# A hybrid diffusion backbone on one core: products over the whole array, and modulation as row sums on VectorE

## Chip, cores and metric

One core of one Trainium2 chip runs the program. The metric is device time in microseconds for one execution; lower is better.

## What is computed

Two layers work on 512 latent tokens and 256 context tokens of 1024 channels. Each layer is modulated by six vectors of 1024 values, made from a conditioning vector c for the latent tokens and c_ctx for the context tokens:

```
mod   = silu(c) @ ada_w + ada_b                    # 6 x 1024, per layer; and with c_ctx
h     = rms_norm(x, g1) * (1 + scale1) + shift1
att   = window_attention(rope(q), rope(k), v, ctx keys and values, sink)
mls   = mlstm_bidir(q, k, v, gates)                # chunks of 128, forward and backward
hy    = hyena(short_conv(u), filters)              # filters: a small network, times exp(-t*delta)
x     = x + gate1 * ((sum_r sigmoid(g_r) * (branch_r @ w_branch_r)) @ w_out)
h2    = rms_norm(x, g2) * (1 + scale2) + shift2
x     = x + gate2 * ((silu(conv3(h2 @ w_up)) * conv3(...)) @ w_down)
```

The last layer needs no context output; there only shift and scale of the first norm are used for c_ctx. The output is a final RMSNorm of the latent tokens.

## The kernel before

Activations lie channel-major, `[128 channels, tokens]`, in eight tiles. Every large matrix product is made of fp32r parts: an operand is split in a high part (ScalarE copies it, line 339) and a low part (VectorE subtracts, line 340), and `kstep` (line 401) issues three matmuls per 128 channels: high by high, high by low, low by high. A weight tile of 128x1024 fp32 (512 KB) comes on the SP queue into one of four buffers `wr` and is split into one of three `wh` and one of three `wl`. The split has raised priority.

**The order of work.** The large products are one stream. Everything else is written as generators ("lanes") that `spawn` adds with a rate; after each `kstep`, `tick` advances a clock and lets each lane take steps in proportion. `finish` runs out what is left at a stage's end. A scheduler then places the instructions of each engine in one fixed order; every engine works through its own in order. Per layer the stages are: projections of the gates (pool `mixa`, with the Hyena filters of layer 0 and the modulation beside them), attention projections and attention beside mLSTM projections (`mix`), mLSTM beside Hyena's projections, Hyena and the merge of the branches (`mixe`), and output projection with the feed-forward part (`ffn`). The filters of layer 1 run in layer 0's feed-forward part. Tiles of two kinds, `T` and `H`, are counted for each stage in `SIZES`.

**Modulation** (`ada`, lines 465 to 490). A block is 512 of the 6144 values. Eight matmuls put two silu vectors (stationary, 32 columns, line 473) against 128x512 of `ada_w`, four groups of channels side by side in the array's columns; ScalarE copies the sum (477), four transposes turn it (481), VectorE adds the groups (484) and the bias (485). There are 12 blocks per layer: four before the first product, eight in layer 0's first projections, nine of layer 1 in layer 0's feed-forward part and three in layer 1's projections.

**Scores** (`scores`, lines 1037 and 1038). For every block of 128 queries and head a product with the key's high part takes all 128 rows (the query's 64 high channels over its 64 low ones); a second one with the key's low part takes the 64 rows of the head's group. An item (a block, two heads, one group; 24 in layer 0 and 16 in layer 1) writes one score tile of three PSUM banks, of which there is one. Masks are added by bf16 products (1049).

**Filter taps** (`filter_taps`, 654 and 655): a product of 128 rows with the high part of w3, and one of 64 rows with its low part. **Decays** (`ml_mix`, 1351 and 1353): two products of 64 rows, with the high and the low part of a running maximum, then a mask.

Of the kernel before, what the change touches and what calls it, by code (L numbers as in the profile page):

```python
# [20 lines left out]
P = 128  # L21
# [11 lines left out]
# order of the m-tiles of the stacked [D_MODEL, 128] weights of a layer  # L33
# [12 lines left out]
# columns of the packed per-channel vectors of a layer  # L46
# [11 lines left out]
# ---------------------------------------------------------------- constants of the shapes  # L58
# [70 lines left out]
# ---------------------------------------------------------------- layout of the inputs  # L129
# [12 lines left out]
def _layout(inp):  # L142
# [7 lines left out]
    out["adaw"] = a["ada_w"].reshape(DEPTH, 4, 2, P, 12, 512).transpose(0, 4, 1, 3, 2, 5).reshape(DEPTH, 12, 4, P, 1024)  # L150
# [88 lines left out]
class Prog:  # L239
# [3 lines left out]
    SIZES = {'A0': (18, 26), 'A1': (8, 41), 'mix': (20, 21), 'E': (16, 29), 'ffn0': (20, 23), 'ffn1': (30, 0)}  # L243
# [12 lines left out]
    ADA1 = 9  # L256
# [4 lines left out]
    def __init__(self, tc, es, aps, dbg=None):  # L261
# [18 lines left out]
        self.nident = c.tile([64, 64], F32R, name="nident")  # L280
        nc.vector.tensor_scalar(self.nident, self.ident[:64, :64], -1.0, None, op0=ALU.mult)
# [6 lines left out]
        self.rope = c.tile([P, 2, SEQ], F32, name="rope")  # L288
# [3 lines left out]
        self.sil = c.tile([P, KD, 32], F32, name="sil")  # L292
        self.g_dram = {}

    def load_consts(self):
        nc, a = self.nc, self.a
        nc.gpsimd.dma_start(self.sv[1], a["sv"][1])
        nc.gpsimd.dma_start(self.fg, a["fg"])
        nc.gpsimd.dma_start(self.rope, a["rope"].rearrange("s p t -> p s t"))
        nc.gpsimd.dma_start(self.maskb, a["masks"])  # L300

    # ---- small helpers
# [39 lines left out]
    # ---- weaving of the mixers' work into the stream of matrix products  # L342
    def spawn(self, rate, *gens):
        lane = Lane(rate, gens)
        lane.t0 = self.clock
# [23 lines left out]
    def fill(self, n):  # L369
        """work put by for the places where the products have to wait"""  # L370
        for _ in range(n):
            next(self.spare, None)

    def finish(self, what=""):
        left = 0.0
        while self.lanes:
            for lane in self.lanes:
                c = lane.step()
                left += c or 0.0
# [4 lines left out]
    # ---- GEMM  # L384
# [34 lines left out]
    def proj_first(self, l, ms, parts):  # L419
        """three m-tiles, part by part, two of them k outermost: the operands may still be coming"""  # L420
# [44 lines left out]
    def ada(self, l, blocks):  # L465
        """blocks of 512 of the six vectors; the groups of k-tiles side by side in the array's columns"""
        nc = self.nc
        for b in blocks:
            ps = self.M("adap")
            for q in range(2):  # L470
                aw = [self.raw(self.a["adaw"][l, b, 2 * q + j]) for j in range(2)]
# [13 lines left out]
            nc.vector.tensor_tensor(m, m, self.svs(l, "adab", b * 4, 4).unsqueeze(2).to_broadcast([P, 4, 2]), op=ALU.add)  # L485
            for i, base in ((1, 0), (2, 24)):
                for h in range(2):
                    if b == (2 if i == 1 else 8) + h:
                        g = self.svs(l, f"n{i}g", 4 * h, 4).unsqueeze(2).to_broadcast([P, 4, 2])
                        nc.vector.scalar_tensor_tensor(self.A[l, i][:, 4 * h:4 * h + 4, :], m, 1.0, g, op0=ALU.add, op1=ALU.mult)  # L490

    # ---- norms
# [56 lines left out]
    # ---- Hyena filters in the frequency domain  # L549
# [20 lines left out]
    def filters(self, l, L, resident, overlap):  # L570
        """spectra of the filters, by order and half of the channels: filter taps, then their DFT"""
# [1198 lines left out]
```

## Time and profile before

| | |
|---|---|
| time, median of 3 runs (lowest to highest) | 2808.58 us (2805.72 to 2810.65) |
| span of the profiled execution | 2804.0 us; its own time is not listed apart |
| TensorE, VectorE, ScalarE, GpSimd busy | 2695.0, 1752.1, 1051.3, 282.1 us |
| weight loads for modulation | 96 of 512 KB |
| moved by DMA | 347.66 MB |

The page gives per engine the time in which it was busy, and lines give groups of instructions by the line of the kernel, with output and inputs by the program's names (`pg` is the PSUM tile of the large products, `wh`, `wl` the weight's parts, `s` scores, `x`, `xl` the parts of queries and keys, `adap`, `adaq` modulation sums). Matmuls overlap, so a busy TensorE is not the same as one at its peak; for what an instruction holds the stream, the distance between two starts in the timeline is read. The kernel's span starts at the first instruction; a run's time includes what lies around it.

### The profile page before, as it was taken

Reading aid. Unit: us, or ns where it says so; the run is one execution under the profiler, and the core shown is the slowest. Engines: PE = TensorE matmul, PEld = TensorE weight load, DVE = VectorE, ACT = ScalarE, POOL = GpSimd, SP = SyncE. Lnnn points to the kernel's source line nnn. Section 1 sums busy time; section 2 is a strip of 40 time slices with the busy share of each in tenths; the row PEclk is TensorE's granted clock in tenths of the full one; section 3 lists DMA queues with packets and bytes.
Section 4 is the critical chain, followed back from the end, with each engine's and each line's share of the span. In section 5 each row is a group of like instructions: output and inputs, shape, how many; then the busy total and the mean of one; then the engine's idle time right before and its main releaser. Section 6 shows DMA issues by size and latency. Waiting matters only on the chain. (4 is left out here: it accounts for less than half of the span.)

```text
span 2804.0 us, 38203 instructions
## 1 busy us (share of the span) xinstructions
PE 2695.0 (96%) x14762; PEld 2199.1 (78%) x14762; DVE 1752.1 (62%) x3076; ACT 1051.3 (37%) x1893; POOL 282.1 (10%) x297
## 2 busy tenths in 40 slices
PE   6899999999999998999999999999999999999998
PEld 2678787778888886787888887777787778888887
DVE  5685554556457765767667566655447477665666
ACT  4344343445323233433233234534345233533333
POOL 3241110000000301011101000210000002000000
PEclk8999999999999999999999999999999999999999
DMA  7555331122436542354443224541222556333332
GB/s 257 168 199 195 108 95 38 38 66 91 151 130 207 174 155 70 116 169 143 132 131 91 68 65 149 185 136 40 76 91 94 185 183 211 98 98 98 97 95 65
DMA packets 153158, 347.66 MB, mean 124 GB/s; under 512 B 15553, under 2 KB 52910, under 8 KB 152976
## 3 DMA queue, kind: packets, MB, share of 16 engines
q1 hardware_dynamic: 132976, 319.03, 34.3%
q0 software_dynamic: 20000, 26.19, 3.7%
q8 instruction: 117, 1.92, 0.3%
q14 instruction: 65, 0.53, 0.1%
HBM read 287.02 MB, written 52.17 MB: 121 GB/s over the span
## 5 line engine op out<-in xcount | busy, mean ns | idle before, releaser
L401 PE MATMUL pg<-hh,wh 128*128 128x512 f32 (+1 forms) x2536 | 923.8, 365 | 7.9 <-ACT hh L339 6.2
L401 PE MATMUL pg<-hlo,wh 128*128 128x512 f32 (+1 forms) x2536 | 900.7, 355 | 4.1 <-DVE hlo L340 3.9
L401 PE MATMUL pg<-hh,wl 128*128 128x512 f32 (+1 forms) x2536 | 898.6, 355 | 0.1
L340 DVE TENSOR_TENSOR wl<-wr,wh 128x1024 fp32r<-128x1024 f32 x294 | 370.3, 1260 | 304.1 <-ACT wh L339 296.2
L401 PEld LDWEIGHTS pg<-hh,wh 128*128 128x128 f32 x2536 | 483.4, 191 | 94.5 <-issue 26.7
L401 PEld LDWEIGHTS pg<-hlo,wh 128*128 128x128 f32 x2536 | 484.3, 191 | 67.2 <-DVE hlo L340 6.8
L401 PEld LDWEIGHTS pg<-hh,wl 128*128 128x128 f32 x2536 | 483.1, 191 | 66.2 <-issue 1.5
L339 ACT CAST wh<-wr 128x1024 fp32r<-128x1024 f32 x294 | 308.8, 1050 | 567.2 <-PE pg L401 525.3
L1527 DVE SCALAR_TENSOR_TENSOR x<-pg,mod,x 128x512 f32<-128x512 f32 (+1 forms) x242 | 149.0, 629 | 113.2 <-PE pg L401 111.0
L401 PE MATMUL pg<-fh,wh 128*128 128x512 f32 (+1 forms) x544 | 194.0, 358 | 8.7 <-DVE x L1527 8.0
L401 PE MATMUL pg<-fl,wh 128*128 128x512 f32 (+1 forms) x544 | 191.6, 352 | 0.0
L401 PE MATMUL pg<-fh,wl 128*128 128x512 f32 (+1 forms) x544 | 190.5, 351 | 0.9 <-DVE wl L340 0.9
L742 ACT ACTIVATE u<-pg,sv 128x512 f32<-128x512 f32 (+1 forms) x165 | 116.6, 708 | 134.9 <-PE pg L401 134.8
L743 DVE SCALAR_TENSOR_TENSOR u<-pg,sv,u 128x511 f32<-128x511 f32 (+1 forms) x165 | 108.3, 658 | 86.2 <-ACT u L742 86.0
L401 PEld LDWEIGHTS pg<-fh,wh 128*128 128x128 f32 x544 | 103.7, 191 | 29.2 <-DVE x L1527 12.1
L1067 ACT ACTIVATE p<-s,sm 128x512 f32<-128x512 f32 (+2 forms) x80 | 55.3, 692 | 171.8 <-DVE sm L1064 142.9
L1063 DVE TENSOR_REDUCE sm<-s 128x1 f32<-128x512 f32 (+2 forms) x80 | 55.2, 690 | 99.5 <-PE s L1049 67.8
L401 PE MATMUL pg<-bh,wh 128*128 128x512 f32 (+1 forms) x320 | 111.7, 381 | 5.6 <-ACT bh L339 3.3
L401 PEld LDWEIGHTS pg<-fh,wl 128*128 128x128 f32 x544 | 103.7, 191 | 15.1 <-DVE wl L340 1.4
L401 PEld LDWEIGHTS pg<-fl,wh 128*128 128x128 f32 x544 | 103.9, 191 | 14.0 <-issue 0.7
L744 DVE SCALAR_TENSOR_TENSOR u<-pg,sv,u 128x511 f32<-128x511 f32 (+1 forms) x165 | 108.7, 660 | 2.5
L401 PE MATMUL pg<-bh,wl 128*128 128x512 f32 (+1 forms) x256 | 94.7, 370 | 0.0
(301 smaller groups left out, 4068.3 us busy)
## 6 DMA issues: line engine op xcount, KB each, us to landing
wr<-in_wA SPq DMA_DIRECT2D x222, 512.0 KB, 3.7
wr<-in_adaw SPq DMA_DIRECT2D x96, 512.0 KB, 4.6
wr<-in_wD SPq DMA_DIRECT2D x48, 512.0 KB, 3.6
wr<-in_wB SPq DMA_DIRECT2D x24, 512.0 KB, 5.2
gates<-gt SPq DMA_DIRECT2D x28, 384.0 KB, 2.7
gc<-in_g POOLq DMA_DIRECT2D x40, 256.0 KB, 3.8
g<-gd SPq DMA_DIRECT2D x40, 256.0 KB, 4.3
g<-gates SPq DMA_DIRECT2D x24, 384.0 KB, 7.7
```

Source lines behind the costliest of these rows:

```text
L339: nc.scalar.copy(h, src)
L340: (nc.gpsimd if pool else nc.vector).tensor_tensor(l, src, h.bitcast(F32), op=ALU.subtract)
L401: self.nc.tensor.matmul(ps[:, :hi - lo], a[:, ks], b[:, lo:hi], start=(first and i == 0), stop=(last and i == 2))
L742: nc.scalar.activation(dst[:, lo:hi], ps[:, :n], AF.Identity, bias=b, scale=w(1))
L743: V(dst[:, lo + 1:hi], ps[:, 0:n - 1], w(0), dst[:, lo + 1:hi], op0=mul, op1=add)
L744: V(dst[:, lo:hi - 1], ps[:, 1:n], w(2), dst[:, lo:hi - 1], op0=mul, op1=add)
L1063: nc.vector.tensor_reduce(sm[:, j:j + 1], src, axis=AX.X, op=ALU.max)
L1067: nc.scalar.activation(t[:, :w], src, AF.Exp, bias=sm[:, 2 + j:3 + j], scale=0.125, accum_out=sm[:, 4 + j:5 + j])
L1527: self.nc.vector.scalar_tensor_tensor(x[m][:, lo:hi], ps[:, :hi - lo], self.mod[l][:, p * 8 + m, j:j + 1], x[m][:, lo:hi], op0=ALU.mult, o ...
```

## The change

Four parts.

*Modulation.* The first four blocks of layer 0 stay as they are. The other 20 use `ada_w` transposed: a tile holds 128 output values as rows of 1024 inputs, and one VectorE instruction per vector multiplies it by silu(c), which stands in all partitions (`silb`), and sums each row into `mod`. Layer 0's blocks and layer 1's first four do so for two vectors, layer 1's last eight for one. The product for the first of two vectors goes into a buffer of tag `wl`, the last one over the tile itself. These lanes stay alive over the stage's ends until the feed-forward part.

*Whole array.* The key's low part is put twice, over both halves of the partitions, as the high part was; the second score product then takes all rows. The taps' second product takes all 128 rows of hd. The maximum's high and low parts share one tile of 128 rows, and `nident` is two negated identities above each other.

*Room.* `silb` takes 8 KB per partition; rope moves from a constant to two `H` tiles that are loaded in each layer's attention projection; `SIZES` gets smaller.

```diff
-    out["adaw"] = a["ada_w"].reshape(DEPTH, 4, 2, P, 12, 512).transpose(0, 4, 1, 3, 2, 5).reshape(DEPTH, 12, 4, P, 1024)
+    out["adaw"] = a["ada_w"][0, :, :2048].reshape(4, 2, P, 4, 512).transpose(3, 0, 2, 1, 4).reshape(4, 4, P, 1024)
+    out["adat"] = a["ada_w"].transpose(0, 2, 1).reshape(DEPTH * 48, P, 1024)[16:]
+    out["cb"] = np.stack([a["c"][0], a["c_ctx"]])
...
-    SIZES = {'A0': (18, 26), 'A1': (8, 41), 'mix': (20, 21), 'E': (16, 29), 'ffn0': (20, 23), 'ffn1': (30, 0)}
+    SIZES = {'A0': (18, 23), 'A1': (8, 38), 'mix': (20, 19), 'E': (16, 27), 'ffn0': (20, 21), 'ffn1': (28, 0)}
...
+        self.nident = c.tile([P, 64], F32R, name="nident")
+        for h in (0, 64):
+            nc.vector.tensor_scalar(self.nident[h:h + 64, :], self.ident[h:h + 64, h:h + 64], -1.0, None, op0=ALU.mult)
...
+    def ada_rows(self, l, blocks):
+        nc = self.nc
+        for b in blocks:
+            n = 2 if l < DEPTH - 1 or b < 4 else 1
+            for c in range(4):
+                aw = self.raw(self.a["adat"][l * 48 + b * 4 + c - 16])
+                for v in range(n):
+                    prod = aw
+                    if v < n - 1:
+                        prod = self.wp.tile([P, 1024], F32R, tag="wl", name=self.uid("wl"), bufs=self.WB[1])
+                    nc.vector.scalar_tensor_tensor(prod, aw, 1.0, self.silb[:, v, :], op0=ALU.mult, op1=ALU.mult,
+                                                   accum_out=self.mod[l][:, b * 4 + c, v:v + 1])
+                if c < 3:
+                    yield 1.0
+            self.ada_end(l, b, n)
+            yield 1.0
+
+    def silu_rows(self):
+        nc = self.nc
+        nc.gpsimd.dma_start(self.silb.rearrange("p v k -> p (v k)"), self.a["cb"].rearrange("v k -> (v k)").partition_broadcast(P))
+        for v in range(2):
+            s = self.silb[:, v, :]
+            t = self.wp.tile([P, 1024], F32, tag="wr", name=self.uid("wr"), bufs=self.WB[0])
+            nc.scalar.activation(t, s, AF.Tanh, scale=0.5)
+            nc.vector.scalar_tensor_tensor(s, t, 1.0, s, op0=ALU.add, op1=ALU.mult)
+            nc.vector.tensor_scalar(s, s, 0.5, None, op0=ALU.mult)
...
-                nc.tensor.matmul(ps, hd[0:64, t * P:(t + 1) * P], w3l[0:64], start=False, stop=True)
+                nc.tensor.matmul(ps, hd[:, t * P:(t + 1) * P], w3l, start=False, stop=True)
...
+        self.rope = [self.H("rope") for _ in range(2)]
+        for i in range(2):
+            self.nc.gpsimd.dma_start(self.rope[i], self.a["rope"][i])
...
         if key:
-            nc.gpsimd.dma_start(top[64:128, :n], top[0:64, :n])
-            nc.gpsimd.dma_start(bot[0:64, :n], bot[64:128, :n])
-            return top, bot, low
+            for a, b in ((top, bot), lows):
+                nc.gpsimd.dma_start(a[64:128, :n], a[0:64, :n])
+                nc.gpsimd.dma_start(b[0:64, :n], b[64:128, :n])
+            return (top, bot), lows
...
-                nc.tensor.matmul(ps[:, o:o + n], qh[ds_, self.chunk(qb)], kl[ds_, ks], start=False, stop=stop)
+                nc.tensor.matmul(ps[:, o:o + n], qh[:, self.chunk(qb)], kl[:, ks], start=False, stop=stop)
...
-                    for x in range(2):
-                        nc.tensor.matmul(pt[:, :w * P], self.nident[:, r:r + 1].to_broadcast([64, P]),
-                                         mn[x][:, i * P:(i + w) * P], start=(x == 0), stop=False)
+                    nc.tensor.matmul(pt[:, :w * P], self.nident[:, r:r + 1].to_broadcast([P, P]),
+                                     mn[:, i * P:(i + w) * P], start=True, stop=False)
...
-                    self.spawn(R["ada"], self.ada(0, range(4, 12)))
+                    self.silu_rows()
+                    self.spawn(1 / 15, self.ada_rows(0, range(4, 12)), stays=True)
...
-                    self.spawn(R["ada"], self.ada(l, range(self.ADA1, 12)))
+                    self.spawn(1 / 11, self.ada_rows(l, range(4, 12)), stays=True)
...
+            self.finish("all")
...
-                    self.spawn(self.RATE[1]["ada"], self.ada(1, range(0, self.ADA1)))
+                    self.spawn(1 / 28, self.ada_rows(1, range(0, 4)))
```

The order in which the engines get their instructions moves with it. On VectorE, in layer 0's first projections, where the second filter's taps (`ht`) are made and the first filter's spectrum (`glo`, `ghi`) is written, the kernel before has this; line 664 starts the next norm of a filter:

```order
L642 TENSOR_TENSOR ht_781<-pm_747,dec_371 128x512
L340 TENSOR_TENSOR wl_890<-wr_887,wh_889 128x1024
L722 TENSOR_TENSOR glo_797<-pe_711,pp_715 128x512
L723 TENSOR_TENSOR ghi_798<-pe_711,pp_715 128x256
L724 TENSOR_TENSOR ghi_798<-pp_715,pe_711 128x256
L642 TENSOR_TENSOR ht_812<-pm_786,dec_373 128x512
```

and the changed one this, at the same place (line 343 is the low part, 681 the taps, 761 to 763 the spectrum, 514 the row sums):

```order
L514 SCALAR_TENSOR_TENSOR wl_672,mod_89<-wr_670,silb 128x1024
L681 TENSOR_TENSOR ht_757<-pm_723,dec_372 128x512
L514 SCALAR_TENSOR_TENSOR wr_670,mod_89<-wr_670,silb 128x1024
L761 TENSOR_TENSOR glo_771<-pe_687,pp_691 128x512
L762 TENSOR_TENSOR ghi_772<-pe_687,pp_691 128x256
L763 TENSOR_TENSOR ghi_772<-pp_691,pe_687 128x256
L343 TENSOR_TENSOR wl_848<-wr_845,wh_847 128x1024
L681 TENSOR_TENSOR ht_786<-pm_762,dec_374 128x512
L514 SCALAR_TENSOR_TENSOR wl_927,mod_89<-wr_925,silb 128x1024
```

The row sums stand one by one between taps, spectrum and the weights' low parts.

On TensorE, in the attention of layer 0, an item's scores were (of the kernel before; `xl` is the key's low part):

```order
L1037 MATMUL s_679_3350<-x_630_3069,x_640_3145 128x256
L1038 MATMUL s_679_3350<-xl_3071,x_640_3145 128x256
L1037 MATMUL s_679_3350<-x_630_3069,x_650_3221 128x256
L1038 MATMUL s_679_3350<-xl_3071,x_650_3221 128x256
L1037 MATMUL s_679_3350<-x_630_3069,x_640_3145 128x256
```

and are now:

```order
L1081 MATMUL s_656_3229<-x_602_2935,x_613_3014 128x256
L1082 MATMUL s_656_3229<-xl_2937,x_613_3014 128x256
L1081 MATMUL s_656_3229<-x_602_2935,x_625_3095 128x256
L1082 MATMUL s_656_3229<-xl_2937,x_625_3095 128x256
L1081 MATMUL s_656_3229<-x_602_2935,x_613_3014 128x256
```

Nothing moves there; only the rows that the second product takes differ, which these lines don't print.

On VectorE near the start of the program, ahead of the first weights' low parts (`wl`), stands in the changed kernel what makes silu:

```order
L495 TENSOR_TENSOR mod_89<-mod_89,sv_85 128x8
L528 SCALAR_TENSOR_TENSOR silb<-wr_462,silb 128x1024
L528 SCALAR_TENSOR_TENSOR silb<-wr_466,silb 128x1024
L529 TENSOR_SCALAR silb<-silb 128x1024 x2
L343 TENSOR_TENSOR w3l_379<-w_99_376,w3h_378 128x512
```

In the kernel before the modulation's bias (485) is followed there by the low part of w3 at once.

## Rows read from the trace of the kernel before

**Rows 1.** Page: busy time of each engine, share of the span, instructions.
```profile
PE 2695.0 (96%) x14762; PEld 2199.1 (78%) x14762; DVE 1752.1 (62%) x3076; ACT 1051.3 (37%) x1893; POOL 282.1 (10%) x297
```

**Rows 2.** Stretches: length; busy us (instructions) of PE, PEld, DVE, ACT, POOL; granted clock; DMA.
```profile
35.00:315.00 280.00, 256.63 (x1387) 187.58 (x1386) 196.67 (x310) 111.86 (x185) 78.54 (x66) 0.94 0.56 189
360.00:595.00 235.00, 234.89 (x1370) 180.22 (x1369) 124.12 (x284) 91.65 (x250) 10.07 (x19) 1.00 0.20 59
1085.00:1735.00 650.00, 633.33 (x3578) 529.58 (x3576) 447.79 (x670) 230.70 (x320) 63.86 (x63) 0.98 0.36 113
```

**Rows 3.** Timeline of TensorE, the stream: start, us, engine, line, operation, tiles, shape, count.
```profile
391.51 0.28 PE L401 MATMUL pg<-hlo,wh 128*128 128x256 f32 x1
391.63 0.28 PE L401 MATMUL pg<-hh,wl 128*128 128x256 f32 x1
...
607.26 0.39 PE L401 MATMUL pg<-hlo,wh 128*128 128x512 f32 x1
607.49 0.40 PE L401 MATMUL pg<-hh,wl 128*128 128x512 f32 x1
```

**Rows 4.** Timeline of TensorE, modulation: products of a half block; transposes.
```profile
1261.90 0.39 PE L401 MATMUL pg<-hh,wl 128*128 128x512 f32 x1
1262.22 1.06 PE L473 MATMUL adap<-wr,sil 128*32 128x512 f32 x8
...
1263.56 0.39 PE L401 MATMUL pg<-hlo,wh 128*128 128x512 f32 x1
...
1281.90 0.28 PE L401 MATMUL pg<-hh,wl 128*128 128x256 f32 x1
1282.02 0.60 PE L481 MATMUL adaq<-ident,adae 128*128 128x128 f32 x4
1282.58 0.28 PE L401 MATMUL pg<-hlo,wh 128*128 128x256 f32 x1
```

**Rows 5.** Timeline of TensorE, scores in layer 0's attention.
```profile
392.43 0.38 PE L1038 MATMUL s<-xl,x 64*128 64x256 f32 x1
392.74 0.39 PE L1037 MATMUL s<-x,x 128*128 128x256 f32 x1
```

**Rows 6.** Groups of TensorE by form: count, busy us, mean ns, idle before.
```profile
L1037 PE MATMUL s<-x,x 128*128 128x256 f32 x112 | 40.5, 361 | 1.5 <-DMA x<-xl 1.4
...
L655 PE MATMUL pm<-w3l,hd 64*128 64x512 f32 x40 | 20.5, 528 | 0.9 <-DVE w3l L340 0.9
...
L1037 PE MATMUL s<-x,x 128*128 128x384 f32 x32 | 13.8, 431 | 0.0
```

**Rows 7.** Timeline of TensorE, a pair of taps in the stream.
```profile
113.73 0.28 PE L401 MATMUL pm<-hh,wl 128*128 128x256 f32 x1
...
114.82 0.28 PE L401 MATMUL pm<-hlo,wh 128*128 128x256 f32 x1
```

**Rows 8.** Timeline of TensorE, a decay in the stream.
```profile
607.81 0.73 PE L1351 MATMUL pm<-mn,nident 64*128 64x512 f32 x2
...
608.94 0.39 PE L401 MATMUL pg<-hlo,wh 128*128 128x512 f32 x1
```

**Rows 9.** Groups of VectorE by form, the nearest to a row sum: mean ns after the bar.
```profile
L340 DVE TENSOR_TENSOR wl<-wr,wh 128x1024 fp32r<-128x1024 f32 x294 | 370.3, 1260 | 304.1 <-ACT wh L339 296.2 <-PE pg L401 2.8 <-ACT o L1126 1.1
...
L1063 DVE TENSOR_REDUCE sm<-s 128x1 f32<-128x640 f32 x32 | 26.4, 824 | 45.0 <-PE s L1049 34.3 <-ACT p L1067 10.7
...
L1599 DVE SCALAR_TENSOR_TENSOR u<-t,u 128x768 f32<-128x768 f32 x22 | 21.4, 971 | 1.6 <-ACT t L1598 1.4
```

**Rows 10.** Groups of ScalarE: the read of an accumulator.
```profile
L1067 ACT ACTIVATION_READ_ACCUMULATOR p<-s,sm 128x1 f32 x80 | 15.7, 196 | 0.0
```

**Rows 11.** Timeline of ScalarE near the start; idle before, what ended it.
```profile
53.56 0.62 ACT L339 CAST w3h<-w 128x512 fp32r<-128x512 f32 x1 [3.48 <-DMA w<-in_hw]
```

**Rows 12.** Waits of TensorE: us in total, times, longest.
```profile
PE adaq L481 <- ACT adae L477: 12.5, 5, 6.0
...
PE pg L401 <- DVE wl L340: 0.9, 1, 0.9
```

More of the change, by code (lines that the diff above doesn't have):

```diff
@@ L255 @@
     NTAIL = 2
-    ADA1 = 9
     ADDS = 6
@@ L287, in __init__ @@
         self.fg = c.tile([P, KD], F32, name="fg")
-        self.rope = c.tile([P, 2, SEQ], F32, name="rope")
         self.maskb = c.tile([P, 2, P], BF16, name="maskb")
@@ L292, in __init__ @@
         self.sil = c.tile([P, KD, 32], F32, name="sil")
+        self.silb = c.tile([P, 2, D], F32, name="silb")
         self.g_dram = {}
@@ L340, in split, with spawn @@
         (nc.gpsimd if pool else nc.vector).tensor_tensor(l, src, h.bitcast(F32), op=ALU.subtract)
-    def spawn(self, rate, *gens):
+    def spawn(self, rate, *gens, stays=False):
         lane = Lane(rate, gens)
+        lane.stays = stays
         lane.t0 = self.clock
@@ L375, in finish @@
         left = 0.0
-        while self.lanes:
+        while any(what == "all" or not x.stays for x in self.lanes):
             for lane in self.lanes:
-                c = lane.step()
-                left += c or 0.0
+                if what == "all" or not lane.stays:
+                    c = lane.step()
+                    left += c or 0.0
             self.lanes = [x for x in self.lanes if x.gens]
@@ L470, in ada @@
             for q in range(2):
-                aw = [self.raw(self.a["adaw"][l, b, 2 * q + j]) for j in range(2)]
+                aw = [self.raw(self.a["adaw"][b, 2 * q + j]) for j in range(2)]
                 for g in range(4):
@@ L484, in ada @@
             nc.vector.tensor_reduce(m, p2.rearrange("p (c g r) -> p c r g", g=4, r=32)[:, :, 0:2, :], axis=AX.X, op=ALU.add)
[L485 to L490, printed above, removed]
+            self.ada_end(l, b, 2)
@@ new lines, in ada_end @@
+    def ada_end(self, l, b, n):
+        nc = self.nc
+        m = self.mod[l][:, b * 4:b * 4 + 4, 0:n]
+        nc.vector.tensor_tensor(m, m, self.svs(l, "adab", b * 4, 4).unsqueeze(2).to_broadcast([P, 4, n]), op=ALU.add)
+        for i in (1, 2):
+            for h in range(2):
+                if b == (2 if i == 1 else 8) + h:
+                    g = self.svs(l, f"n{i}g", 4 * h, 4).unsqueeze(2).to_broadcast([P, 4, n])
+                    nc.vector.scalar_tensor_tensor(self.A[l, i][:, 4 * h:4 * h + 4, 0:n], m, 1.0, g, op0=ALU.add, op1=ALU.mult)
@@ L776, in att_finish @@
         self.att["q"].append(self.stacked(self.att_last[0], self.parts(l)[-1][1], False))
+        self.rope = None
     def rope_swap(self, q):
@@ L787, in rope_add @@
         nc = self.nc
-        nc.gpsimd.tensor_tensor(r, r, self.rope[:, 1, :], op=ALU.mult)
-        nc.vector.tensor_tensor(q[:, :SEQ], q[:, :SEQ], self.rope[:, 0, :], op=ALU.mult)
+        nc.gpsimd.tensor_tensor(r, r, self.rope[1], op=ALU.mult)
+        nc.vector.tensor_tensor(q[:, :SEQ], q[:, :SEQ], self.rope[0], op=ALU.mult)
         nc.vector.tensor_tensor(q[:, :SEQ], q[:, :SEQ], r, op=ALU.add)
@@ L796, in stacked @@
         top, bot, low = self.T("x0", dt=F32R), self.T("x1", dt=F32R), self.T("xl", dt=F32R)
-        for h, t in ((0, top), (64, bot)):
+        lows = (low, self.T("xm", dt=F32R)) if key else (low, low)
+        for h, t, lw in ((0, top, lows[0]), (64, bot, lows[1])):
             nc.scalar.copy(t[h:h + 64, :n], x[h:h + 64, :n])
-            nc.vector.tensor_tensor(low[h:h + 64, :n], x[h:h + 64, :n], t[h:h + 64, :n].bitcast(F32), op=ALU.subtract)
+            nc.vector.tensor_tensor(lw[h:h + 64, :n], x[h:h + 64, :n], t[h:h + 64, :n].bitcast(F32), op=ALU.subtract)
         if key:
-            nc.gpsimd.dma_start(top[64:128, :n], top[0:64, :n])
-            nc.gpsimd.dma_start(bot[0:64, :n], bot[64:128, :n])
-            return top, bot, low
+            for a, b in ((top, bot), lows):
+                nc.gpsimd.dma_start(a[64:128, :n], a[0:64, :n])
+                nc.gpsimd.dma_start(b[0:64, :n], b[64:128, :n])
+            return (top, bot), lows
         nc.gpsimd.dma_start(top[64:128, :n], low[0:64, :n])
@@ L1313, in ml_load @@
             self.ml[name] = t
-        self.ml["mn"] = [self.T("mn", [64, NT], F32R) for _ in range(2)]
+        self.ml["mn"] = self.T("mn", [P, NT], F32R)
         for x in range(2):
-            nc.gpsimd.dma_start(self.ml["mn"][x], self.mld[0:64, 2 + x, :])
+            nc.gpsimd.dma_start(self.ml["mn"][64 * x:64 * x + 64, :], self.mld[0:64, 2 + x, :])
     def small(self, s):
```

7 lines of the change are left out of this document (2 added, 5 removed).

## The prediction

> **What bounds the kernel now.** I began with the table of engine totals. TensorE is busy for 96% of the span, VectorE for 62% [rows 1]. [...] Only the first projections (35 to 315) have slack, 256.63 of 280 us. VectorE has 196.67 of those 280 us, 124.12 of 235 in attention, 447.79 of 650 in the feed-forward part. So TensorE's stream of products sets the end, nearly everywhere, and what matters is how long each inserted piece holds that stream. The third view, TensorE's timeline, tells this by the distance from one start to the next; the durations of matmuls overlap and are no use here. Two 256-column products of like shape start 0.12 us apart, two of 512 columns 0.23 us [rows 3].
>
> **What the change removes from TensorE.**
>
> *Modulation.* Half a block, eight narrow products, takes from 1261.90 to 1263.56, with two products of the stream in it [rows 4]: 1.66 - 2 x 0.23 = 1.20 us. The four transposes of a block take from 1281.90 to 1282.58 with two 256-column products: 0.68 - 0.24 = 0.44 us. A block is 2 x 1.20 + 0.44 = 2.84 us, and 20 blocks are **57 us**. Eight of them lay in the first projections, nine in layer 0's feed-forward part, three in layer 1's projections.
>
> *Scores.* A score product and its 64-row partner start 0.31 us apart, either way, against 0.12 us for two products of like shape [rows 5]. The stream pays 0.19 us for each change between half the array's rows and all of them. There are 2 x (112 + 32) = 288 such matmuls [rows 6], but the first of each of the 40 items follows a whole-array product and pays half of that. 248 x 0.19 + 40 x 0.09 = **51 us**. I take the 384-column ones at the same surcharge. The masks' products stay as they are. That the partner now multiplies 128 rows costs nothing: a product's spacing follows its columns, and the stream's products have 128 rows too.
>
> *Taps.* A pair in the stream, from 113.73 to 114.82, holds two 512- and two 256-column products [rows 7]: 1.09 - 0.46 - 0.24 = 0.39 us too much; 40 pairs [rows 6] are **16 us**.
>
> *Decays.* From 607.49 to 608.94 lie one product of the stream, two 64-row products, a mask and the next one [rows 3, 8]: 1.45 us. One whole-array product in place of two leaves four of 0.23 us, 0.92 us. That saves 0.53 us for each of 16 pairs of 512 columns (four heads, two directions, two layers); for layer 0's eight pairs of 256 columns I estimate 0.3 us. Together **11 us**.
>
> In all 57 + 51 + 16 + 11 = **135 us**.
>
> **What it adds to VectorE.** Layer 0's eight blocks are 8 x 4 x 2 = 64 row sums, layer 1's first four blocks 32 and its last eight (one vector) 32: 128 row sums of 128x1024. No such instruction with an accumulated output is in the trace. The nearest rows: a tensor_tensor of 1024 elements takes 1260 ns, a scalar_tensor_tensor with both sources in SBUF 971 ns for 768 [rows 9], so without the sum 1.26 us is its price, and the lower end. ScalarE's accumulating exponential is followed by a read of its accumulator of 196 ns [rows 10]; I add as much, as an estimate. That gives 1.46 us, 187 us in all, and a VectorE of (1752 + 187) / 2690 = 72%. The upper end is a product and a reduction one after the other: a reduction of 640 takes 824 ns, so some 1.22 us for 1024, and 2.48 us in all. I take the lower price because the plain form with two fp32 sources, the nearest row, runs at full rate [rows 9].
>
> [...]
>
> **Where that shows.** *First projections:* twelve modulation tiles, so 24 row sums (35 us), and silu's four instructions (4 us) come onto 196.67 us; some 2 us of the old way's reductions go. That is 234 us in a stretch that shrinks by 8 x 2.84 + 24 taps x 0.39 = 32 us to 248: 94%. The two row sums of a tile stand in VectorE's order among taps and spectra, and taps are products on TensorE that wait for them. I give back 12 of the 32 us (bounds: none and all). *Start:* silu waits for a 1 MB broadcast on POOL's queue behind the x loads, and its two results, four instructions of VectorE, stand ahead of the first weights' low parts. ScalarE stood 3.48 us there, waiting for w3 [rows 11], which covers the two tanh; VectorE's part I price at 4 us, as the third weight's buffer is released by it. *Attention of both layers:* a pair of row sums per some 15 us adds 2.92 us there: layer 0's 124.12 us become 170 in about 205 us. The chain from scores through maximum, exponential and the single scores buffer becomes a little later; 4 us. *Buffers:* 3, 3, 2, 2 and 2 fewer tiles for filters and Hyena, two fewer at the end: 5 us, no row prices it; bounds 0 and 15. *At nothing:* rope's load, now at the start of each attention projection, hidden behind the key's projection and its swap, 4 us late if that cover is gone; two more copies of the keys' low parts on POOL's queue, hidden behind four query projections; 96 modulation loads of 512 KB stay 96, on the same SP queue and the same four buffers. But a weight's load now waits for a row sum on VectorE where it waited for TensorE, and the first product of each pair takes one of three buffers for low parts. Behind it on VectorE stand the next weight's low part and the conversions of taps.
>
> **The sum.** 2804.0 - 135 + (12 + 4 + 4 + 5) = 2694 us of span. The runs' median, 2808.58, lies 4.6 us above this span, which holds the launch around it and the scatter of the runs (5 us); the profiled execution's own time is not given apart. So **2699 us**, 3.9% less.
>
> **The rivals.**
>
> *All of it counts.* VectorE's extra work hides everywhere. For it: TensorE waited once, 0.9 us, for a low part of a weight of this stream, while VectorE stood 296 us waiting for ScalarE's halves [rows 9, 12], so it has time ahead. Of TensorE's 12.5 us of waits for copied modulation sums [rows 12] some 7 go too, an estimate. 2804 - 135 - 7 + 5 = 2667 us.
>
> *VectorE becomes the bound.* At the upper price a row sum takes 2.48 - 1.46 = 1.02 us more: first projections 24 x 1.02 = 24 us on 234, more than their 248, so that stage's remaining 20 us go and 10 more; layer 0's attention 15 tiles, 31 us on 170 in 205 us, full, 12 us; 5 us in the feed-forward part. 2699 + 30 + 12 + 5 = 2746 us. [...]
>
> *Slower than before: the row sums block VectorE.* The first product of a pair writes a low-part buffer and must wait until TensorE has left the weight three before; VectorE stands meanwhile, and the next weight's low part behind it comes late. 48 tiles do this (layer 0 and the feed-forward part). It decides once TensorE loses 110 / 48 = 2.3 us at each. A wait for half a weight's latent product (24 x 0.23 = 5.5 us) gives 48 x 2.75 = 132 us, so 2699 + 132 = 2831 us. Against it: VectorE comes early to the low parts now, and waits for ScalarE's halves [rows 9].
>
> *No effect,* since another engine's chain sets the time as soon as TensorE's shrinks: 2809 us. The dense windows [rows 2] speak against it.
>
> **How the numbers follow.** Forecast 0.56 (2675 to 2730); all counts 0.12; VectorE bound 0.24 (2730 to 2790); blocked 0.06; no effect 0.02. The range leaves out the last two and the worst of the bound VectorE: 2660 to 2768. A measurement can tell 0.2% (6 us) from no change: faster 0.56 + 0.12 + 0.24 = 0.92, the same 0.02, slower 0.06.
>
> **What would show it.** Right: score products 0.12 us apart in attention, no narrow products after the first four blocks, a row sum of 1.2 to 1.5 us, VectorE near 72% and TensorE still above 95%; attention of layer 0 nearly 25 us shorter. Wrong: a row sum above 2 us; in the first projections VectorE above 95% and waits of TensorE for VectorE of tens of us; low parts of weights waited for at every modulation tile; or scores still 0.3 us apart, in which case what costs is not the change of rows.

## The result and the profile after

The changed kernel takes 2729.93 us (median of 4 runs, 2726.24 to 2732.05), the kernel before 2807.82 us in the same comparison: ratio 0.9723, 95% interval 0.9709 to 0.9736. It is 78 us faster where 110 were forecast. The profiled execution has a span of 2724.2 us against 2804.0, so 79.8 us less.

The table of engine totals, to be held against [rows 1]:

```profile
PE 2570.0 (94%) x14338; PEld 2171.1 (80%) x14338; DVE 1890.5 (69%) x3317; ACT 1039.2 (38%) x1874; POOL 298.9 (11%) x305
```

TensorE has 424 matmuls less: 20 blocks of 20 and 24 decays. It is busy for 125 us less, but also a smaller share of a shorter span, 94% in place of 96: it waits more. VectorE gained 138 us. The groups of VectorE show what a row sum is (the columns are instructions, then busy us and mean ns, then the idle time ahead and what ended it):

```profile
L514 DVE SCALAR_TENSOR_TENSOR wr<-wr,silb 128x1024 f32<-128x1024 f32 x80 | 98.3, 1229 | 36.8 <-DMA wr<-in_adat 36.4
L514 DVE SCALAR_TENSOR_TENSOR wl<-wr,silb 128x1024 fp32r<-128x1024 f32 x48 | 60.4, 1259 | 29.0 <-PE pg L406 23.7 <-PE pm L406 5.0
L514 DVE DVE_READ_ACCUMULATOR wr<-wr,silb 128x1 f32 x80 | 6.5, 82 | 0.0
L514 DVE DVE_READ_ACCUMULATOR wl<-wr,silb 128x1 f32 x48 | 3.9, 82 | 0.0
```

One takes 1.23 to 1.26 us and a read of the accumulator 0.08 us more: 1.32 us, 169 us in all. The second row also shows the wait that the prediction feared: VectorE stood 29 us until TensorE had left a low-part buffer (line 406 is the product that line 401 was). Who pays for it stands in the waits of TensorE (us in total, times, longest):

```profile
PE pm L899 <- DVE fold L888: 13.6, 10, 4.3
PE pp L749 <- DMA gc<-in_g: 11.3, 3, 8.8
...
PE pm L1487 <- DVE hs L1478: 10.4, 8, 1.9
PE pm L899 <- issue: 7.8, 2, 5.9
...
PE pg L406 <- ACT gt L1512: 6.0, 2, 4.0
PE adaq L486 <- ACT adae L482: 5.4, 3, 3.9
...
PE pg L406 <- DVE wl L343: 1.2, 2, 0.9
```

For low parts of weights TensorE waits 1.2 us, hardly more than before [rows 12], so nothing is lost to that. At the top now stand the folded inputs of Hyena (line 888; 8.2 us before), the matrices of the filters' DFT (`gc`; none before), the mLSTM's normalized output (`hs`, 1478; 5.5 before) and a gate's PSUM tile (1512; none before). Two lines that are left out above, the high parts of operands (`hh`) and the residual (`x`), went from 6.2 to 11.0 us and from 8.2 to 10.5. The wait for copied modulation sums (486) fell from 12.5 to 5.4 us.

Scores are as forecast: on TensorE's timeline they start 0.12 us apart, where it was 0.31 [rows 5]:

```profile
487.92 0.28 PE L1081 MATMUL s<-x,x 128*128 128x256 f32 x1
488.04 0.28 PE L1082 MATMUL s<-xm,x 128*128 128x256 f32 x1
488.15 0.28 PE L1081 MATMUL s<-x,x 128*128 128x256 f32 x1
488.27 0.28 PE L1082 MATMUL s<-xm,x 128*128 128x256 f32 x1
```

By stretches (length; busy us of PE, PEld, DVE, ACT, POOL; clock; DMA), the first projections, layer 0's attention and its feed-forward part, as [rows 2]:

```profile
35.00:305.00 270.00, 227.44 (x1224) 182.94 (x1213) 213.32 (x332) 107.57 (x175) 86.25 (x65) 0.92 0.47 153
350.00:556.00 206.00, 205.47 (x1355) 170.41 (x1354) 140.82 (x317) 91.80 (x249) 13.04 (x24) 1.00 0.32 91
1045.00:1670.00 625.00, 605.07 (x3414) 526.51 (x3412) 481.05 (x721) 228.21 (x314) 66.06 (x64) 0.98 0.34 101
```

Attention shrank from 235 to 206 us, the feed-forward part from 650 to 625, both nearly full as before. The first projections shrank by 10 us only, and TensorE's slack there rose from 23 to 43 us. From its first product to the end of the stage (the first row of the table below), the kernel before, the changed one, and e10, an experiment that issues the same instructions as the changed one up to there:

```profile
59.30:354.40 295.10, 277.76 (x1540) 215.21 (x1539) 195.77 (x297) 106.76 (x174) 77.53 (x64) 0.96 0.51 168
59.60:344.40 284.80, 250.58 (x1382) 210.91 (x1381) 218.28 (x331) 100.88 (x164) 86.76 (x66) 0.96 0.43 140
59.10:348.10 289.00, 254.25 (x1381) 214.63 (x1380) 219.71 (x331) 100.67 (x164) 86.45 (x66) 0.94 0.43 137
```

The change took 27 us of busy time off TensorE here, and 17 of them came back as idle time: 17 us before, 34 after.

To see stage by stage who won what, I count the products of the stream (there are 10872 in every kernel, in the same stages) and compare when the same product starts in each trace. The table gives the change against the kernel before within each stage, in us; the columns of the experiments belong to the next section.

| stage, to product | after | e1 arrays | e2 rows | e3 sizes | e4 narrow | e7 hybrid | e10 even | e11 both |
|---|---|---|---|---|---|---|---|---|
| first projections, 1050 | -10.1 | -6.1 | -5.8 | +5.3 | -9.4 | +1.2 | -6.3 | -13.2 |
| layer 0's attention, 1830 | -31.1 | -28.9 | -3.9 | 0.0 | -29.0 | -29.0 | -31.4 | -31.0 |
| its mLSTM and Hyena, 3400 | +2.9 | -3.1 | +10.5 | -1.4 | -3.4 | -4.0 | +6.9 | +5.3 |
| most of its feed-forward part, 5600 | -28.6 | -5.1 | -23.1 | -0.8 | -29.1 | -31.5 | -25.3 | -23.2 |
| the rest, layer 1's projections, 7400 | -2.7 | +0.9 | -3.6 | -0.3 | -6.3 | -2.0 | -8.2 | -8.8 |
| layer 1's attention, 8000 | -17.7 | -21.7 | +8.1 | -0.8 | -21.1 | -15.2 | -21.3 | -21.7 |
| its mLSTM and Hyena, 8800 | +8.6 | -1.2 | +8.7 | +0.7 | +0.8 | +9.4 | -1.0 | -0.4 |
| to the end | -1.1 | -0.6 | -0.8 | -0.1 | +0.3 | -1.3 | -0.5 | +0.4 |
| span | -79.8 | -65.8 | -9.8 | +2.6 | -97.1 | -72.3 | -87.1 | -92.6 |

How far one execution may be trusted: the changed kernel and e10 issue the same instructions in the same order to past product 3400, and yet differ by 3.8 us in the first projections and by 4.0 us in layer 0's mLSTM and Hyena. The rows above tell why: TensorE is idle as long in both, 34 and 35 us, but the granted clock is 0.96 in one and 0.94 in the other. By the clock's records 25 us of the first projections had a granted clock of 0.5 in the changed kernel and 37 in e10, and so had 10 and 24 us of layer 0's mLSTM and Hyena. So a difference of 4 us in one stage is read as an effect only where several kernels show it, or where TensorE's idle time, which hardly depends on this, shows it too.

### The profile page after: what moved, and what is told of

Same layout as the page of the kernel before. It is cut to its first block, busy times and chain, and to the rows that moved or that the text cites. A ratio compares the mean times of both kernels' runs of the same rounds, so it can differ in the third digit from the quotient of the medians.

```text
span 2724.2 us, 37645 instructions
## 1 busy us (share of the span) xinstructions
PE 2570.0 (94%) x14338; PEld 2171.1 (80%) x14338; DVE 1890.5 (69%) x3317; ACT 1039.2 (38%) x1874; POOL 298.9 (11%) x305
## 5 line engine op out<-in xcount | busy, mean ns | idle before, releaser
L406 PE MATMUL pg<-hh,wh 128*128 128x512 f32 (+1 forms) x2536 | 916.6, 362 | 21.1 <-ACT hh L342 11.0
L406 PEld LDWEIGHTS pg<-hh,wh 128*128 128x128 f32 x2536 | 484.4, 191 | 87.2 <-ACT hh L342 12.5
L342 ACT CAST wh<-wr 128x1024 fp32r<-128x1024 f32 x294 | 308.8, 1050 | 615.0 <-PE pg L406 580.4
L514 DVE SCALAR_TENSOR_TENSOR wr<-wr,silb 128x1024 f32<-128x1024 f32 x80 | 98.3, 1229 | 36.8 <-DMA wr<-in_adat 36.4
```

Of the source, the lines that this page charges most:

```text
L342: nc.scalar.copy(h, src)
L406: self.nc.tensor.matmul(ps[:, :hi - lo], a[:, ks], b[:, lo:hi], start=(first and i == 0), stop=(last and i == 2))
L514: nc.vector.scalar_tensor_tensor(prod, aw, 1.0, self.silb[:, v, :], op0=ALU.mult, op1=ALU.mult, accum_out=self.mod[l][:, b * 4 + c, v:v + 1])
```

## The experiments

Three theories stood at the start. *VectorE:* the row sums stand among short chains that TensorE waits for. *Pools:* the missing gain is the smaller pools. *Size:* the terms of the sum were too large.

**The parts apart.** e1 puts scores, taps and decays alone into the kernel before; e2 the modulation with its pools and rope; e3 only these:

```diff
-    SIZES = {'A0': (18, 26), 'A1': (8, 41), 'mix': (20, 21), 'E': (16, 29), 'ffn0': (20, 23), 'ffn1': (30, 0)}
+    SIZES = {'A0': (18, 23), 'A1': (8, 38), 'mix': (20, 19), 'E': (16, 27), 'ffn0': (20, 21), 'ffn1': (28, 0)}
...
-        nc.gpsimd.dma_start(self.rope, a["rope"].rearrange("s p t -> p s t"))
...
+        self.rope = [self.H("rope") for _ in range(2)]
+        for i in range(2):
+            self.nc.gpsimd.dma_start(self.rope[i], self.a["rope"][i])
```

> The kernel before with the scores, taps and decays alone on the whole array; modulation, pools and rope as before. If the terms of the sum are of the right size and only the row sums give time back (VectorE theory) or the smaller pools do (pool theory): 78 us less than before, about 2730 us (2724 to 2738). If these three terms were too large (size theory; the distances from start to start in the changed kernel's trace save some 65 us): 2743 us or more.

> The kernel before with the 20 modulation blocks as row sums on VectorE, the smaller pools and rope's late load; scores, taps and decays as before. VectorE theory: 57 us come off TensorE and some 25 to 30 go back as TensorE's waits in the first projections and in layer 1, about 2780 us (2773 to 2787). Pool theory: the same kernel with the same pools, also about 2780 us. Size theory (the three other terms were too large, this one is whole): 2751 to 2762 us.

> The kernel before with nothing but the smaller pools and rope loaded late into two tiles of the pool. Pool theory: 15 to 25 us slower than before, 2823 to 2833 us. VectorE and size theory: within 5 us of before, as the prediction's 5 us for the buffers has it, 2803 to 2813 us.

e1 took 2740.66 us, ratio 0.9777 (0.9760 to 0.9794): 63 us by the ratio in place of 78. The time lies between the two ranges, the gain next to the size theory's 65 us. e2 took 2795.24 us, 0.9965 (0.9952 to 0.9978): 10 us, less than any theory gave it. e3 took 2811.1 us, 1.0019 (1.0009 to 1.0028): 5 us slower, the pools' price in the prediction and no more. The table shows where: e3 loses 5.3 us in the first projections and nothing behind them. e1's 51 us in the two attentions, nearly the scores' alone (four of the 24 decays stand there too), are whole; taps bring 6.1 + 5.1 and decays 3.1 + 1.2 us. e1 and e2 add to 72 us, the changed kernel has 78, so the parts hardly disturb each other, and the question is the modulation.

**VectorE's time.** e4 is the changed kernel with short row sums:

```diff
-                    nc.vector.scalar_tensor_tensor(prod, aw, 1.0, self.silb[:, v, :], op0=ALU.mult, op1=ALU.mult,
+                    nc.vector.scalar_tensor_tensor(prod[:, :16], aw[:, :16], 1.0, self.silb[:, v, :16], op0=ALU.mult, op1=ALU.mult,
```

> The changed kernel with each row sum over 16 of the 1024 columns: it leaves out the rest of the modulation's sums for 20 blocks and keeps every load, buffer and wait. VectorE theory: the time that the row sums cost comes back, 2700 to 2710 us. Pool and size theory: no more than 5 us comes back, 2724 to 2730 us.

2709.12 us, ratio 0.9658 (0.9645 to 0.9671): some 18 us come back by the ratios (0.9723 - 0.9658 of 2808), so the row sums cost something. (The scheduler also moved some TensorE instructions, so the single microseconds are not the row sums' alone.) But the table says where: nothing in the first projections (-9.4 against -10.1), nothing in most of the feed-forward part; 6.3 us in layer 0's mLSTM and Hyena (without row sums there e1, e4 and e7 all have -3 to -4, with them the changed kernel, e10 and e11 +3 to +7), 3.6 in layer 1's projections, 3.4 in its attention, 7.8 in its mLSTM and Hyena. By TensorE's idle time in these four it is 4.5, 1.8, 2.0 and 4.7 us, 13 in all; the rest lies in busy time, in which the clock counts (in the rows above 250.58 us at 0.96 and 254.25 at 0.94). In 105 to 210 us, the densest of the first projections, VectorE of the changed kernel is busy 95%:

```profile
105.00:210.00 105.00, 95.97 (x565) 81.44 (x565) 99.33 (x152) 36.11 (x56) 45.06 (x30) 1.00 0.46 152
```

and of e4 86%:

```profile
105.00:210.00 105.00, 94.09 (x539) 81.44 (x540) 90.15 (x156) 40.76 (x64) 34.57 (x30) 0.95 0.44 151
```

and TensorE did not get further. Its clock was lower in that window of e4, 0.95 against 1.00, so the whole stage decides:

```profile
60.10:345.00 284.90, 249.57 (x1381) 212.29 (x1380) 195.15 (x331) 101.17 (x164) 73.40 (x66) 0.95 0.42 139
```

TensorE is idle for 35 us, where the changed kernel has 34. A full VectorE was beside the point there. In mLSTM and Hyena it was not. TensorE's waits from 2100 to 2290 us in the changed kernel:

```profile
PE pm L899 <- DVE fold L888: 6.1, 3, 4.3
PE pm L899 <- issue: 5.9, 1, 5.9
```

and in e4, from 2090 to 2270 us, the same stage:

```profile
PE pm L899 <- issue: 6.0, 1, 6.0
...
PE pm L899 <- DVE fold L888: 0.9, 1, 0.9
```

With short row sums the longest of these waits, 4.3 us, becomes 0.9. But the fold itself is no later in the changed kernel. From the last accumulation before it to its transposes, in the changed kernel:

```profile
2190.93 0.28 PE L1020 MATMUL acc<-dc,zl 128*128 128x256 f32 x1
...
2191.52 0.39 PE L406 MATMUL pg<-hh,wl 128*128 128x512 f32 x1
2196.18 0.30 PE L899 MATMUL pm<-ident,fold 128*128 128x128 f32 x1 [4.27 <-DVE fold L888]
```

and in e4:

```profile
2171.67 0.28 PE L1020 MATMUL acc<-dc,zl 128*128 128x256 f32 x1
...
2175.67 0.39 PE L406 MATMUL pg<-hh,wl 128*128 128x512 f32 x1
2176.97 0.57 PE L899 MATMUL pm<-ident,fold 128*128 128x128 f32 x2 [0.92 <-DVE fold L888]
```

Both take 5.3 us, VectorE does the same work in both, and the last row sum of the changed kernel had begun 34 us before these transposes. What differs is the cover: TensorE has 3 products in between in the changed kernel and 18 in e4. The row sums moved the place of the transposes in TensorE's order, and the products that could cover this wait had been issued ahead of it (8640 products of the stream stand before it, 8631 in e4).

In layer 0's mLSTM and Hyena it is another link. The changed kernel, from 558 to 978 us:

```profile
PE pm L899 <- DVE fold L888: 7.5, 7, 2.0
PE pm L1487 <- DVE hs L1478: 5.8, 4, 1.9
```

and e4, from 561 to 974 us:

```profile
PE pm L899 <- DVE fold L888: 7.5, 5, 3.4
PE pm L1487 <- DVE hs L1478: 2.7, 4, 1.1
```

The fold's waits are the same, those for the mLSTM's output are halved; only the longest of them, 1.9 us, had a row sum on VectorE in the 8 us before it. In both places TensorE transposes what VectorE has made a moment before. How much of the price is VectorE's time and how much the order that came with the row sums is not shown: no run shortened them in the changed kernel's order.

**The row sums elsewhere.** Layer 1's 32 row sums for its last eight blocks can be done any time after the start. e5 moves them to layer 0's feed-forward part, behind those that are there; e10 gives them a second lane beside the first:

```diff
 e5
-                    self.spawn(1 / 11, self.ada_rows(l, range(4, 12)), stays=True)
...
-                    self.spawn(1 / 28, self.ada_rows(1, range(0, 4)))
+                    self.spawn(1 / 10.5, self.ada_rows(1, range(0, 12)))
 e10
-                    self.spawn(1 / 11, self.ada_rows(l, range(4, 12)), stays=True)
...
                     self.spawn(1 / 28, self.ada_rows(1, range(0, 4)))
+                    self.spawn(1 / 16, self.ada_rows(1, range(4, 12)))
```

> The changed kernel with all 48 modulation tiles of layer 1 (64 row sums) in layer 0's feed-forward part, none in layer 1. VectorE theory (row sums cost time where TensorE waits for short chains of VectorE, in layer 1's mixers, and nothing in the feed-forward part): some 12 us less than the changed kernel, 2714 to 2722 us, with the gain between layer 1's projections and its merge. Rival (the row sums cost the same wherever they stand): 2726 to 2733 us.

> As the run with all of layer 1's modulation in layer 0's feed-forward part, but in two lanes side by side, so that the tiles with two row sums no longer come close together at its start. Density theory (that run lost 10 us in the feed-forward part since two row sums per tile crowded VectorE in its first third): 4 to 7 us faster than that run, 2718 to 2722 us. Rival (64 row sums cost the feed-forward part 10 us however they are spread): 2724 to 2729 us.

e5: 2725.62 us, ratio 0.9703 (0.9690 to 0.9716). From layer 1's projections to its merge 18 us were gained, where the forecast had some 12 in all, but the feed-forward part gave 10 us of it back, so the time lies just between the two ranges. e10: 2719.0 us, 0.9686 (0.9665 to 0.9706), the density theory's figure: spread evenly, the row sums that came into this part cost most of it (to product 5600) 3 us, and 5 and 4 in e11 and e12, where 10 were lost in e5. 20 of the 32 stand there, 26 in e5; the others, in the rest of the part, cost nothing that the table shows. VectorE is busy for 81% of that time, as in e5, against 77% in the changed kernel:

```profile
1045.00:1670.00 625.00, 604.06 (x3426) 524.37 (x3424) 507.74 (x779) 223.58 (x306) 67.85 (x63) 0.99 0.42 127
```

In layer 1's Hyena, 2100 to 2290 us, the waits for the fold are nearly gone, as in e4:

```profile
PE pm L899 <- issue: 3.6, 1, 3.6
...
PE pm L899 <- DVE fold L888: 1.5, 2, 0.9
```

So what a row sum costs is decided by where it stands, its stage and its neighbours, and not by VectorE's share.

**The first projections.** They kept 22 of the 32 us, and VectorE is not why. e6 gives some pools back what memory is left; e7 puts layer 0's last eight blocks onto TensorE again, where they were before; e8 and e9 spread the filters' work wider:

```diff
 e6
+    SIZES = {'A0': (18, 25), 'A1': (8, 40), 'mix': (20, 19), 'E': (16, 28), 'ffn0': (20, 22), 'ffn1': (28, 0)}
 e7
-                    self.spawn(1 / 15, self.ada_rows(0, range(4, 12)), stays=True)
+                    self.spawn(R["ada"], self.ada(0, range(4, 12)))
 e8, and e9 with 1.52
-    RATE = ({'filt': 1.587, 
+    RATE = ({'filt': 1.45, 
```

> The changed kernel with two more tiles in layer 0's first pool (25), two more in layer 1's first (40), one more for Hyena (28) and one in layer 0's feed-forward part (22); nothing else. Pool theory (the waits of TensorE for the loads of the DFT matrices in the first projections are waits for a free tile): 4 to 8 us less, 2721 to 2726 us, with these waits of 11.3 us gone and the first projections that much shorter. Rival (what is left of the stage's length is the filters' chain of engines, whatever the pool): within 3 us, 2727 to 2733 us.

> The changed kernel with layer 0's last eight modulation blocks as narrow products on TensorE again, at the old place in the first projections; layer 1's blocks stay row sums. Chain theory (in the first projections TensorE waits for the filters' chain, so that the narrow products there were mostly free): the stage becomes 3 to 7 us longer, layer 0's mixers 4 us shorter without row sums, 2728 to 2735 us in all. Size theory (eight blocks at 2.84 us each are paid there in full): 2744 to 2750 us.

> The changed kernel with the filters' work in layer 0's first projections spread wider: 1.45 in place of 1.587 us of it per us of products, so that it ends with the stage's last products and not 10 per cent before. Chain theory: more products lie between the links, TensorE waits less, 3 to 8 us gained, 2722 to 2727 us. Rival (the waits are for free tiles or for loads): within 3 us of the changed kernel, 2727 to 2733 us.

> The changed kernel with the filters of layer 0's first projections at 1.52 in place of 1.587 us of work per us of products (1.45 let the products run 10 us ahead in the middle of the stage and lost 18 us at its end, waiting for the last spectra). Chain theory (the stage's length is set by how the filters' chain is laid into the products, not by TensorE's or VectorE's load): between the two the waits in the middle shrink and the end is not late, 4 to 10 us gained, 2720 to 2726 us. Rival (TensorE's and VectorE's load sets it): within 3 us of the changed kernel, 2727 to 2733 us.

e6: 2724.94 us, 0.9703 (0.9690 to 0.9717). Some 5 us, in the first projections. e11 (below), which differs from e10 in its pools alone, gains 6.9 there and e3 lost 5.3, so pools are a part of it. The waits for the DFT's matrices, which fell from 11.3 to 7.7 us, do not show that by themselves: in e10, with the changed kernel's pools, they are 2.7. e7: 2735.49 us, 0.9738 (0.9724 to 0.9751): only 5.6 us more, just above the chain theory's range. The stage became 11.3 us longer, not 3 to 7, for eight blocks, 22.7 us by the prediction's price, and layer 0's mixers won 6.9 back. TensorE is busy for 21 us more there and idle for 10 us less: half of what the narrow products took had been taken while TensorE would have waited anyway. TensorE's waits from 59 to 345 us name for whom, here in the changed kernel:

```profile
PE pp L749 <- DMA gc<-in_g: 11.3, 3, 8.8
PE pg L406 <- ACT gt L1512: 6.0, 2, 4.0
PE pp L749 <- ACT sdh L342: 4.3, 7, 2.3
PE pm L693 <- ACT w3h L342: 3.3, 3, 1.5
PE pm L700 <- POOL ab L689: 3.2, 4, 1.1
```

All but the second are links of the filters' chain (taps, their sums, their high parts, the DFT), which goes through every engine. The longest, 8.8 us, stands where the kernel before had its 6.0 us for a copied modulation sum [rows 12]: the place of the wait had another name, and the wait stayed. How little the name says, e10 shows with the same instructions:

```profile
PE pp L749 <- ACT sdh L342: 12.5, 6, 8.6
...
PE pp L749 <- DMA gc<-in_g: 2.7, 3, 1.8
```

Its 8.6 us stand before the same product as the 8.8, and here the high part of the taps' sums (`sdh`) came last.

e8 is a miss: 2737.53 us, 0.9748 (0.9734 to 0.9761), 8 us slower. In the middle its products ran up to 11 us ahead of the changed kernel's, as forecast, but the last spectra then stood alone at the end:

```profile
325.38 0.39 PE L406 MATMUL pg<-hh,wl 128*128 128x512 f32 x1
330.49 0.58 PE L749 MATMUL pp<-sdh,gc 128*128 128x256 f32 x1 [4.71 <-ACT sdh L342]
...
339.18 0.58 PE L406 MATMUL pg<-hh,wh 128*128 128x256 f32 x1 [4.48 <-ACT k L773]
```

e9 is the next miss: 2732.99 us, 0.9736 (0.9715 to 0.9756), at the upper end of the rival's range. A small lead in the middle, a small loss at the end, no gain.

**The two edits that gained, and the filters earlier.** e11 has e10's lanes and e6's pools; e12 the same with the filters at 1.68.

> The two edits that gained, together: layer 1's modulation in two lanes in layer 0's feed-forward part (10.9 us less than the changed kernel by the medians) and the larger pools (5.0 us less). If they act in different stages, as the traces say, they add: 2730 - 16 = 2714 us (2711 to 2718). If the pools' gain was the scatter of the first projections: 2718 to 2723 us.

> As the run before it, with the filters of layer 0's first projections at 1.68 in place of 1.587 us of work per us of products, so that they begin each link earlier. Chain theory in its narrow form (the end of the filters' chain sets the end of the first projections; 1.52 and 1.45 put it later): 3 to 8 us less than that run, 2706 to 2711 us. Rival (the stage's length stays where it is, since an earlier link is waited for in the middle instead of at the end): within 3 us of that run, 2711 to 2717 us.

e11: 2713.21 us, 0.9661 (0.9644 to 0.9677). The two add, and this version beats both kernels, 17 us under the changed one by the medians. e12: 2723.16 us, 0.9697 (0.9683 to 0.9712), 10 us worse than e11, against both theories: in its first projections the matrices are waited for 10.7 us, 7.5 in e11, and the sums of the taps 8.6, 4.4 in e11:

```profile
PE pp L749 <- DMA gc<-in_g: 10.7, 3, 8.4
PE pm L700 <- POOL ab L689: 8.6, 7, 2.8
```

Of the 13.5 us that the stage lost against e11, 8 are TensorE's idle time; most of the rest is clock, with 46 us at a granted clock of 0.5 in place of 32. So the theory that the end of the filters' chain alone sets the stage's end has fallen; begun earlier, the chain is waited for before its end. What is shown is this: products taken out win half their time there or less, VectorE time taken out wins none, larger pools win some 5 us, and no other pace of the filters that was tried, 1.45, 1.52 or 1.68, wins anything. That the rest is set by how this chain is laid between the products fits all of it, but is argued: the three forecasts made from it, e8, e9 and e12, missed. Which link could be shortened with profit stays open; no run tried that.

## Why the prediction was right, and where it was wrong

Direction and range were right, and so was the mechanism wherever TensorE's stream was full; the forecast was 31 us low, and by the table this comes from the gross sum, not from the give-backs. That 2729.93 still falls into the forecast's own band, 2675 to 2730, is luck: it lies 0.07 us inside its end. Two signs came out otherwise: TensorE is busy for 94%, not above 95, and layer 0's attention is 31 us shorter, not 25.

*Scores: right.* 51 us forecast; e1 has 28.9 + 21.7 in the two attentions. A change between 64 and 128 rows costs what the spacing of 0.31 against 0.12 us said, 0.19 us; what TensorE does in that time, no run here shows.

*Taps and decays: right in kind, too large.* For the taps 16 us were forecast and 11 measured, for the decays 11 and 4. "1.09 - 0.46 - 0.24 = 0.39" was read from one pair. Over the 34 pairs at a granted clock of 1.00 with no wait beside them, a pair with the delay of the product behind it holds the stream for 0.68 us before and 0.39 after: 0.29 saved, 12 us for 40. The same count gives 0.36 us for a decay of 512 columns and 0.29 for one of 256, 8 us in all; that the table shows 4 lies within the scatter of its stages, and four decays are counted under attention.

*Modulation: the step that failed.* "A block is 2 x 1.20 + 0.44 = 2.84 us, and 20 blocks are 57 us" took every block for stream time. Nine blocks in the feed-forward part were worth 28.6 - 5.1 = 23.5 us (after less e1; 25.6 forecast). In e4, which has no row sums to speak of, layer 1's three were worth 6.3 + 0.9 = 7 (8.5 forecast). Eight in the first projections were worth 10.1 - 6.1 = 4, or 9 without the pools' 5; 22.7 were forecast. The window [rows 2] showed 23 us of slack in that stage, and still every block was priced in full there. After the first product TensorE had waited 10 us for the filters' chain and 7 for copied modulation sums, and with the blocks gone its idle time there went from 17 to 34 us.

*Give-backs: 25 us forecast, some 22 measured (17 for row sums by the spans of e4 and the changed kernel, 5 for pools), in other places.* That their sum is nearly right is luck. "I give back 12 of the 32 us" was put down to row sums between taps and spectra: e4 shows none. Silu: the first product starts at 59.6 us in place of 59.3, so 0 and not 4 us. Pools: 5 and 5, in the first projections alone. "Attention of both layers ... 4 us": by e4 the row sums cost nothing in layer 0's and 3 in layer 1's, but 14 in mLSTM and Hyena of both layers and 4 in layer 1's projections, for which the prediction had no term. Nobody had asked what comes late next in these stages: the mLSTM's output in layer 0, the fold in layer 1.

*Row sums: right.* 1.46 us forecast with a read of the accumulator, 1.32 measured; VectorE 69% against 72. The instruction itself took 1229 and 1259 ns for 1024 fp32 values, the time of the plain difference of two such tiles, 1260 [rows 9]. "Runs at full rate" was the author's word for such times, here 1.20 and 1.23 ns a value against 1.26 in the row of 971 ns; no row shows VectorE's highest rate. So the rival of the bound VectorE fell by its price, 1.32 us where it had 2.48, although the time, 2730, is just where its range began. VectorE did reach 95% in a part of the first projections, a sign that was to show this rival; e4 shows that it was not the cause. Over the stage it was 79% (213.32 of 270 us), where 94 were forecast.

*The blocked VectorE* had its waits (29 us for buffers) and no price: TensorE waited 1.2 us for low parts. *All counts* and *no effect* were not near.

## What to carry to other kernels

Before work is taken off the busy engine, split its price by stage: where that engine has slack in a window, work removed there was partly cover for a chain through other engines, and comes back as waits under a new name (here about half of 23 us). Work added to another engine is priced by what stands behind it and by how it moves the order, not by that engine's share: 32 row sums cost 3 to 5 us when spread through a dense stage in which VectorE then ran at 81%, and some 15 in layer 1, half of that where TensorE transposes what VectorE has just made. Look there at TensorE's order, too: a chain that is no slower is waited for longer when fewer products stand in front of its result (4.3 us behind 3 of them, 0.9 behind 18). Counting the same product in both traces, stage by stage, shows where to look, and the idle time and the granted clock of the stage show how much of a difference is scatter.

## What the runs showed of the hardware

The accumulated output cost VectorE a second instruction of 82 ns, and nothing in the first one: 1229 and 1259 ns for 1024 values in the mean, and 1219 and 1220 with no GpSimd work beside it, where the plain difference of two such tiles takes 1222.

The clock scatters between executions of the same instructions: e10 and the changed kernel differ by 4 us in a stage of 285 to 289 us with equal idle time, at a granted clock of 0.94 and 0.96.

VectorE itself ran slowly before the fold that TensorE waited 4.3 us for. Its timeline in the changed kernel:

```profile
2192.80 1.83 DVE L343 TENSOR_TENSOR wl<-wr,wh 128x1024 fp32r<-128x1024 f32 x1
2194.55 1.48 DVE L888 TENSOR_TENSOR fold<-u 128x256 f32<-128x256 f32 x1
2195.96 0.41 DVE L889 TENSOR_TENSOR fold<-u 128x256 f32<-128x256 f32 x1
```

and of GpSimd:

```profile
2192.29 3.46 POOL L1052 TENSOR_TENSOR y<-y,x 128x512 f32<-128x512 f32 x2 [86.22 <-DVE y L1051]
```

The first takes 1.83 us where 263 of its 294 kind, those with no GpSimd work beside them, take 1.22 (none over 1.23); the second 1.48 where the third, alike, takes 0.41. Both ran while GpSimd worked. Of the other 31 of that kind, 20 took no longer; the 11 slow ones, 1.25 to 2.31 us, all began while a tensor_tensor of GpSimd ran, and ended 1.08 or 1.09 us after it. Those that began first were not held up: they took 1.16 to 1.23 us. What the two engines wait for there, no run shows. It is not what sets the changed kernel apart: in the kernel before, in e4 and in e10 the same fold takes 1.50 us beside GpSimd, and TensorE waits 0.9 us for it.
